# A two-layer decoder trunk on one core: another order of the input, sums of squares in pairs, and a scheduler with three rules more

## The chip, the cores and the metric

The kernel runs on one core of one Trainium2 chip. TensorE (PE in the profile) multiplies matrices and writes into PSUM, eight banks of 512 fp32 values in each of 128 partitions; VectorE (DVE), ScalarE (ACT) and GpSimd (POOL) work on tiles in SBUF, the first two also on PSUM; SyncE (SP) issues the DMA transfers between HBM and SBUF. The engines run side by side, each through its own list of instructions in order, and wait for one another through semaphores. The metric is the device time of one execution in microseconds, as a median of several runs.

## The reference

The input x has 512 rows of 1024 values. Two layers follow one another, then a final RMSNorm. What matters here is the beginning of a layer; the mixers are named alone:

```python
def hybrid_layer(x, c_silu, ...):
    mod = c_silu @ w_ada + b_ada
    shift, scale, gate = jnp.split(mod, 3, axis=-1)
    u = rms_norm(x, norm_g) * (1 + scale[:, None]) + shift[:, None]
    z = u @ w_in
    ...
    ya = dsa_attention(...) * jax.nn.silu(ag)             # indexer, top 128 keys, softmax
    yb = swa_sinks_attention(...) * jax.nn.silu(bg)       # sliding window
    yc = stick_breaking_attention(...) * jax.nn.silu(cg)
    merged = (jax.nn.sigmoid(ma) * (ya @ w_br_a) + jax.nn.sigmoid(mb) * (yb @ w_br_b)
              + jax.nn.sigmoid(mc) * (yc @ w_br_c))
    return x + gate[:, None] * (merged @ w_out)
```

All of it is fp32. z has 8,772 columns per layer.

## The kernel before

**Layout.** Everything is kept transposed: features on the 128 partitions, the 512 rows of x (positions) along the free dimension. x is eight tiles k = 0 to 7 of 128 x 512. A product in fp32 precision is made of three faster ones: each operand is split into a high part (type fp32r) and the low rest, and hi x hi, hi x lo, lo x hi are summed in PSUM. So a weight chunk `wstage` from HBM becomes `whi` (a cast) and `wlo` (a subtraction), and u becomes `uh` and `ul`. `cast` may run on ACT, VectorE or, from SBUF, POOL; `both` (a tensor_tensor) on VectorE or POOL; a line with one engine's name is bound to it.

**Stages of a layer.** `first_phase` multiplies u by the first seven column tiles of w_in (`FIRST`, 896 columns), all seven banks open at once while k runs from 0 to 7: 7 x 3 products per k. `v_phase` makes the value columns. Then several streams are woven into one order: `prep_stream` (the other projections), `mixer_c`, `mixer_ab`, `indexer` and `topk`, `fill_stream` (gates and branch products), `ada_stream` (the next modulation). `out_phase` closes the layer, its last two tiles in two halves of 256 columns.

**The start of layer 0** (`start`, lines 1467 to 1523) loads x in two halves of columns (`norm`): four transfers of two tiles each, then ACT squares them two at a time and 8 products with a matrix of -1 sum the squares over the partitions, which gives -1 times the sum of squares in all partitions; `rstd_of` makes the root through Ln and Exp on ACT, in place in the same PSUM bank. Order of SP's list: small vectors, first half of x, w_ss of k = 0 (`ada_load(0)`, two pieces of 512 KB into Y), the two weight chunks of k = 0, second half of x, w_ss of k = 1, chunks 2 and 3, w_ss of k = 2. `busy` adds products without use that keep TensorE's clock up. Shift and scale of k come from `ada_first(k)`: VectorE multiplies each piece by silu(c), spread over all partitions in `csr`, and sums it along the row; `linear` makes `mods` and `amul`. `times_rstd` (VectorE) multiplies x by the root, `make_u` writes `uh` and a full-precision copy (tile e), both by ACT in layer 0, and `ul` as their difference. The first item of `first_phase` (`two0`) takes k = 0 and 1 together, each in halves of columns, and for each of the seven tiles hi x uh, hi x ul, lo x uh.

**The order.** Nothing of this is emitted at once. Every call is recorded (`Recorder.add`) with its dependencies, taken from overlapping ranges of tiles, and a price for each engine that may run it (`price`). `forward` then builds the whole order as a list scheduler: at each step the engine and the instruction that can start first, ties by due time; `elsewhere` passes an instruction by on one engine when another would end it sooner. `latest` works the due times out backwards from that order. `order` does this five times, each round with the due times of the one before, keeps the round whose modelled end is earliest, and `emit` writes it out. Each engine's instructions keep that order on the chip; the framework adds the semaphores, and it keeps accesses of two engines to one PSUM bank apart whether or not their ranges overlap.

Of the kernel before, what the change touches and what calls it, by code (L numbers as in the profile page):

```python
# [25 lines left out]
F32 = mybir.dt.float32  # L26
# [6 lines left out]
S = 512  # L33
# [216 lines left out]
class Instr:  # L250
    __slots__ = ("i", "alts", "writes", "reads", "preds", "succs", "left", "est", "tiles", "start", "end", "prio", "bound", "engine", "taken", "hold")
# [7 lines left out]
class Recorder:  # L259
# [34 lines left out]
    def add(self, ways):  # L294
        x = Instr()
        x.i = len(self.list)
        op, args, kw = next(iter(ways.values()))
        if op == "pairs":
            named = [(("out", "in", "in")[n], v) for q in args for n, v in enumerate(q[:3])]
            opened = {id(q[0]) for q in args if q[3]}  # L300
        else:
            named = [("out" if "out" not in kw and n == 0 else n, v) for n, v in enumerate(args)] + list(kw.items())
        x.writes = [v for n, v in named if isinstance(v, View) and n in ("out", "accum_out")]
        x.reads = [v for n, v in named if isinstance(v, View) and n not in ("out", "accum_out")]
        x.preds, x.succs = {}, []
        for views, w in ((x.reads, False), (x.writes, True)):
            for v, r in [(v, r) for v in views for r in v.regions()]:
                t = v.tile
                if w and (op == "matmul" and kw["start"] or op == "pairs" and id(v) in opened):
                    r = (r[0], r[1], 0, S)  # L310
                keep = []
                for (j, r2, w2) in t.seen:
                    over = r[0] < r2[1] and r2[0] < r[1] and r[2] < r2[3] and r2[2] < r[3]
                    if over and j is not x and (w or w2):
                        x.preds[j.i] = j
                    if not (w and over and r[0] <= r2[0] and r2[1] <= r[1] and r[2] <= r2[2] and r2[3] <= r[3] and j is not x):
                        keep.append((j, r2, w2))
                t.seen = keep + [(x, r, w)]
        x.tiles = list({id(v.tile): v.tile for v in x.reads + x.writes if not v.tile.pool.fixed}.values())
        for j in x.preds.values():  # L320
            j.succs.append(x)
        x.alts = {}
        for e, (op, args, kw) in ways.items():
            x.alts[e] = self.price(x, e, op, args, kw)
        x.prio = x.i
        self.list.append(x)

    def price(self, x, engine, op, args, kw):
# [67 lines left out]
        y.cost, y.lag = c - self.OVERLAP[engine], c  # L396
        return y


    def forward(self):  # L400
# [3 lines left out]
        for x in self.list:  # L404
            x.left, x.est, x.bound, x.taken = len(x.preds), 0.0, len(x.tiles), False
            for t in x.tiles:
                waiting.setdefault(id(t), []).append(x)
# [6 lines left out]
        def offer(x):  # L414
            if x.left == 0 and x.bound == 0:
                for e in x.alts:
                    heapq.heappush(E[e]["pend"], (x.est, x.i))
# [20 lines left out]
        while len(out) < len(self.list):  # L438
            best = None
            for name, e in E.items():  # L440
# [29 lines left out]
                if mine is not None:  # L470
                    asked = max(free, self.list[mine[2]].est)
                    if best is None or (mine[0], asked, mine) < best[:3]:
                        best = (mine[0], asked, mine, name)
# [43 lines left out]
    def elsewhere(self, x, name, at, E):  # L517

        end = at + x.alts[name].cost
        for o, y in x.alts.items():  # L520
            if o != name:
                t = max(E[o]["free"], at, E[o]["port"] if y.port else 0.0) + y.cost
                if t < end - 1e-9:
                    return True
        return False

    def latest(self, end, out):
# [11 lines left out]
        for x in reversed(out):  # L539
# [4 lines left out]
            if x.engine in after:  # L544
                v = min(v, late[after[x.engine]] - x.hold)
# [59 lines left out]
def trunk(ctx, tc, xT, vecs, w_ss, w_gt, w_first, w_t, w_v, w_br, w_o, rope, consts, out):  # L605
# [146 lines left out]

    def ada_load(j):
        st["wada", j] = [rec.tile("Y", [P, 2 * S], F32) for _ in range(2)]
        for i in range(2):
            SP.dma_start(st["wada", j][i].rearrange("p (a b) -> p a b", a=2), w_ss[0, j, 2 * i:2 * i + 2].rearrange("q p s -> p q s"))
# [54 lines left out]
    def make_u(l, k, xk, cs_=FULL):  # L811
# [5 lines left out]
        for o in (st["uh"][k][:, cs_], t):  # L817
            if l == 0:
# [56 lines left out]
    def stack_q(r, scale=None, sbuf=True):  # L875
        q = rec.tile("Q", [P, 2, S], F32R)
        for e, (a, b) in enumerate(((H0, H1), (H1, H0))):
            if scale is None:
                cast(q[a, e], r[a])
                both(q[b, e], r[a], f(q[a, e]), OP.subtract)  # L880
            else:
                cast(q[a, e], r[a], scale)
# [12 lines left out]
    def stack_k(r, sbuf=True):  # L895
        kh, kl = new_kh(), klow[st["nk"] % 2]
        st["nk"] += 1
        for e, (a, b) in enumerate(((H0, H1), (H1, H0))):
            cast(kh[a, e], r[a])
            cast(kh[b, e], f(kh[a, e]))  # L900
            both(kl[a, :S], r[a], f(kh[a, e]), OP.subtract)
# [50 lines left out]
    def first_phase(l):  # L952
# [19 lines left out]

        def two(*w):
# [493 lines left out]
    def start():  # L1467
# [9 lines left out]
        for h in range(2):  # L1477
# [4 lines left out]
            ACT.activation(csr[:, S * h:S * h + S], p, AF.Copy, scale=-1.0)  # L1482
# [5 lines left out]
        nb = st["nbank"] = st["rstd"] = sbank()  # L1488

        def norm(cs_):  # L1490
            for k in range(0, KT, 2):
                SP.dma_start(xx[k // 4][:, k % 4:k % 4 + 2, cs_], xT[:, k:k + 2, cs_])
            for k in range(0, KT, 2):
                t = t512("t", 10)
                ACT.activation(t.rearrange("p (a b) -> p a b", a=2), xx[k // 4][:, k % 4:k % 4 + 2, cs_], AF.Square)
                for i in range(2):
                    mm(nb[:, cs_], f(nones), t[:, 256 * i:256 * i + 256], cs_.start == 0 and k + i == 0, k + i == 7)
            rstd_of(nb[:, cs_])
# [5 lines left out]
        norm(HALVES[0])  # L1504
        ada_load(0)
        ch.load(1)
# [15 lines left out]
        ch.load(3)  # L1522
# [114 lines left out]
```

## Time and profile before

| | us |
|---|---|
| median of 3 runs | 1181.68 (1181.54 to 1181.86) |
| profiled execution | 1180.98 |
| its span, first to last instruction | 1179.1 |
| mean granted TensorE clock | 0.998 |
| SP's transfers, issue to landing, w_ss pieces of 512 KB | 6.2 |
| SP's transfers, issue to landing, weight chunks of the first projection | 4.4 |

All times of instructions count from the start of the span. In the rows of the profile a line reads: program line, engine, operation, the tile written and the tiles read, shapes, count; then busy microseconds and mean nanoseconds of one, then the engine's idle time before these instructions and what ended it. Nearly all instructions have line 577, since one place emits them, so groups are told apart by tile names: `uh`, `ul`, `whi`, `wlo`, `wstage`; `Y` holds w_ss in the start; `vc` and `va` hold x there; `t` holds squares in the start and softmax tiles later; `ps_z` and `ps_s` are PSUM banks (3 and 5); `small` holds the small vectors. One fp32 product with the matrix of -1 shows as two records.

### The profile page before, as it was taken

Reading aid. Unit: us, or ns where it says so; the run is one execution under the profiler, and the core shown is the slowest. Engines: PE = TensorE matmul, PEld = TensorE weight load, DVE = VectorE, ACT = ScalarE, POOL = GpSimd, SP = SyncE. Lnnn points to the kernel's source line nnn. Section 1 sums busy time; section 2 is a strip of 40 time slices with the busy share of each in tenths; the row PEclk is TensorE's granted clock in tenths of the full one; section 3 lists DMA queues with packets and bytes.
Section 4 is the critical chain, followed back from the end, with each engine's and each line's share of the span. In section 5 each row is a group of like instructions: output and inputs, shape, how many; then the busy total and the mean of one; then the engine's idle time right before and its main releaser. Section 6 shows DMA issues by size and latency. Waiting matters only on the chain.

```text
span 1179.1 us, 17734 instructions
## 1 busy us (share of the span) xinstructions
PE 1166.5 (99%) x6006; PEld 967.9 (82%) x6006; DVE 988.1 (84%) x2275; ACT 532.0 (45%) x1127; POOL 111.8 (9%) x160
## 2 busy tenths in 40 slices
PE   9999999999999999999999999999999999999997
PEld 8899777788878887788899987777888888877886
DVE  6977999999999887787587689999997988667765
ACT  6523667653455532632143147775443653234222
POOL 1100333310000000000000014332100000000000
PEclk9999999999999999999999999999999999999999
DMA  9644323334444454245533432333342333322343
GB/s 354 219 119 120 90 81 86 95 107 125 121 116 126 130 143 143 81 141 153 166 113 108 128 101 72 90 87 119 99 132 83 90 98 100 107 72 88 93 125 106
DMA packets 81914, 139.39 MB, mean 118 GB/s; under 512 B 10016, under 2 KB 22560, under 8 KB 81824
## 3 DMA queue, kind: packets, MB, share of 16 engines
q1 hardware_dynamic: 80672, 136.17, 39.5%
q10 hardware_dynamic: 1152, 2.10, 0.5%
q8 instruction: 47, 0.77, 0.3%
q14 instruction: 43, 0.35, 0.1%
HBM read 125.39 MB, written 4.19 MB: 110 GB/s over the span
## 4 chain that ended last, share of the span: by engine, by line
PE 81%; DVE 13%; ACT 2%; issue 2%; DMA 1%; SPq 0%; DVEq 0%; ACTq 0%
PE ps_z L577 61%; PE ps_s L577 16%; DVE t L577 5%; PE ps_s L575 4%; DVE score L577 2%; ACT t L577 1%; DVE m L577 1%; DVE wlo L577 1%; DVE Q L577 1%; DVE klow L577 1%; DMA Y<-in_w_ss 1%; DVE Y L577 0%; DVE wstage L577 0%; ACT KH L577 0%; ACT e L577 0%
## 5 line engine op out<-in xcount | busy, mean ns | idle before, releaser
L577 PE MATMUL ps_z<-uh,whi 128*128 128x512 f32 (+1 forms) x908 | 357.4, 394 | 0.0
L577 PE MATMUL ps_z<-uh,wlo 128*128 128x512 f32 (+1 forms) x908 | 353.4, 389 | 0.0
L577 PE MATMUL ps_z<-ul,whi 128*128 128x512 f32 (+1 forms) x908 | 352.5, 388 | 0.0
L577 DVE TENSOR_TENSOR wlo<-wstage,whi 128x512 fp32r<-128x512 f32 (+2 forms) x321 | 210.4, 659 | 11.0 <-ACT whi L577 2.3
L577 PEld LDWEIGHTS ps_z<-uh,whi 128*128 128x128 f32 x908 | 170.5, 188 | 35.2 <-issue 1.9
L577 PEld LDWEIGHTS ps_z<-uh,wlo 128*128 128x128 f32 x908 | 170.6, 188 | 34.6 <-issue 0.9
L577 PEld LDWEIGHTS ps_z<-ul,whi 128*128 128x128 f32 x908 | 170.7, 188 | 32.6 <-issue 0.7
L577 DVE CAST whi<-wstage 128x512 fp32r<-128x512 f32 (+2 forms) x224 | 91.3, 408 | 106.6 <-PE ps_z L577 87.5
L577 PE MATMUL ps_z<-Y,whi 128*128 128x512 f32 x384 | 119.3, 391 | 0.0
L577 ACT CAST whi<-wstage 128x512 fp32r<-128x512 f32 (+2 forms) x105 | 63.2, 602 | 109.9 <-PE ps_z L577 82.3
L577 ACT ACTIVATE e<-ps_z 128x512 f32<-128x512 f32 x68 | 40.3, 592 | 135.9 <-PE ps_z L577 135.7
L577 POOL TENSOR_TENSOR wlo<-wstage,whi 128x512 fp32r<-128x512 f32 (+2 forms) x51 | 64.8, 1271 | 382.7 <-ACT whi L577 143.8
L577 ACT ACTIVATE e<-e 128x512 f32<-128x512 f32 x96 | 59.8, 629 | 53.3 <-DVE e L577 52.8
L577 PEld LDWEIGHTS ps_z<-Y,whi 128*128 128x128 f32 x384 | 71.7, 188 | 14.7
L577 ACT ACTIVATE t<-t,nm 128x256 f32<-128x256 f32 (+3 forms) x128 | 65.1, 510 | 35.5 <-DVE nm L577 35.5
L577 PE MATMUL ps_z<-Y,wlo 128*128 128x512 f32 x192 | 74.7, 389 | 0.0
L577 ACT ACTIVATE t<-t 128x512 f32<-128x512 f32 x120 | 68.2, 625 | 13.3 <-DVE t L577 12.5
L577 PEld LDWEIGHTS ps_s<-small,t 128*128 128x128 f32 x432 | 48.8, 140 | 16.2 <-DVE t L577 5.1
L577 PE MATMUL ps_s<-small,t 128*128 128x128 f32 x432 | 58.2, 275 | 3.6 <-DVE t L577 2.5
L577 DVE MAX8 m<-score 128x8 f32<-128x256 f32 (+2 forms) x96 | 53.3, 556 | 1.1
L577 PE MATMUL ps_s<-KH,Q 128*128 128x256 f32 (+3 forms) x280 | 52.4, 309 | 0.2
L577 DVE MATCH_REPLACE8 score<-m,score 128x256 f32<-128x256 f32 (+2 forms) x96 | 52.1, 543 | 0.1
(202 smaller groups left out, 1951.5 us busy)
## 6 DMA issues: line engine op xcount, KB each, us to landing
wstage<-in_w_t SPq DMA_DIRECT2D x212, 256.0 KB, 2.7
wstage<-in_w_v SPq DMA_DIRECT2D x48, 182.0 KB, 2.4
Y<-in_w_ss SPq DMA_DIRECT2D x16, 512.0 KB, 6.2
m<-zs SPq DMA_DIRECT2D x128, 64.0 KB, 2.0
wstage<-in_w_gt SPq DMA_DIRECT2D x32, 256.0 KB, 2.6
wstage<-in_w_ss SPq DMA_DIRECT2D x32, 256.0 KB, 2.7
wstage<-in_w_o SPq DMA_DIRECT2D x32, 256.0 KB, 2.7
wstage<-in_w_first SPq DMA_DIRECT2D x16, 256.0 KB, 4.4
```

What stands on the lines that cost most here:

```text
L575: self.real[engine].matmul(*[real(a) for a in q[:3]], start=q[3], stop=True, skip_group_check=True)
L577: made = getattr(self.real[engine], y.op)(*[real(a) for a in y.args], **{k: real(v) for k, v in y.kw.items()})
```

## The change

The start loads x whole, ahead of everything but the small vectors, in five transfers (2, 2, 2, 1 and 1 tiles); then w_ss of k = 0 (the second piece as two of 256 KB), then chunks 0 and 1. The squares of tiles 0 and 1, of 2 and 3, and of 4, 5 and 6 are added up elementwise before a product sums them; tile 7 goes alone, and the last two sums run in halves of columns. k = 0 is still made in halves, k = 1 whole. In `two0` the products of k = 0 go by term (hi x uh for all seven tiles, then hi x ul, then lo x uh), and k = 1 in full width.

In the recorder three rules come in. Two accesses to one PSUM bank, one of TensorE and one of another engine, now depend on each other even if their ranges don't overlap; two accesses by ACT and VectorE to one bank are kept in their recorded order and, across engines, apart (`after`, `apart`, `soft`). An ACT or VectorE instruction on fewer than 128 partitions is priced as holding its engine for its whole length and a little more. Due times no longer follow the next instruction on the same engine except on PE and SP. `elsewhere` asks when the other engine could start the instruction, rather than from the present one's time on; the modelled landing of early transfers is sooner; and in `stack_q` and `stack_k` the casts are recorded ahead of the subtractions. For k = 0 of layer 0 `make_u` may use VectorE too, and so may the copy into `csr`.

```diff
@@ Recorder.add
+        mine = next(iter(ways)) == "PE"
...
+                bank = t.pool.name[:3] == "ps_"
                 for (j, r2, w2) in t.seen:
                     over = r[0] < r2[1] and r2[0] < r[1] and r[2] < r2[3] and r2[2] < r[3]
-                    if over and j is not x and (w or w2):
+                    if j is not x and (w or w2) and (over or bank and mine != ("PE" in j.alts)):
                         x.preds[j.i] = j
+                    elif j is not x and bank and not mine and "PE" not in j.alts:
+                        x.after[j.i] = j
@@ price
         y.cost, y.lag = c - self.OVERLAP[engine], c
+        if engine != "POOL" and o.shape[0] < P:
+            y.cost = c + (0.08 if engine == "DVE" else 0.02)
@@ forward
-                x.end = dma_free = max(at + 3.0, dma_free) + y.lag * (1.6 if dma_free < 5.5 else 1.0)
+                x.end = dma_free = max(at + (2.1 if at < 20.0 else 3.0), dma_free) + y.lag * (1.2 if dma_free < 5.5 else 1.0)
...
+            for s in x.apart:
+                for o in s.alts:
+                    if o != name:
+                        s.soft[o] = max(s.soft.get(o, 0.0), x.end + self.NEXT)
+                s.left -= 1
+                offer(s)
@@ elsewhere
-                t = max(E[o]["free"], at, E[o]["port"] if y.port else 0.0) + y.cost
+                t = max(E[o]["free"], x.est, x.soft.get(o, 0.0), E[o]["port"] if y.port else 0.0) + y.cost
@@ latest
+            for s in x.apart:
+                v = min(v, late[s.i] - (x.hold if s.engine == x.engine else took + self.NEXT))
-            if x.engine in after:
+            if x.engine in after and x.engine in ("PE", "SP"):
                 v = min(v, late[after[x.engine]] - x.hold)
@@ ada_first
             w = st["wada", j][i]
+            if i > j:
+                for q in range(2):
+                    c = slice(S * q, S * q + S)
+                    DVE.scalar_tensor_tensor(w[:, c], w[:, c], 1.0, csr[:, c], op0=OP.mult, op1=OP.mult, accum_out=o[:, 2 + q:3 + q])
+                DVE.tensor_tensor(out=o[:, 1:2], in0=o[:, 2:3], in1=o[:, 3:4], op=OP.add)
+                continue
@@ make_u
-            if l == 0:
+            if l == 0 and k:
                 ACT.activation(o, xk[:, cs_], AF.Identity, scale=sc, bias=sh)
                 continue
@@ first_phase
+        def terms(w, cs_):
+            fb = st["first"]
+            uh, ul = st["uh"][0][:, cs_], st["ul"][0][:, cs_]
+            for n, v in ((0, uh), (0, ul), (1, uh)):
+                for i in range(NF):
+                    c = slice(128 * (i % 4), 128 * (i % 4) + 128)
+                    mm(fb[i][:, cs_], w[i // 4][n][:, c], v, cs_.start == 0 and n == 0 and v is uh, False)
...
         def two0(*w):
-            for k in (0, 1):
-                for cs_ in HALVES:
-                    mms(k, w[2 * k:2 * k + 2], cs_)
+            for cs_ in HALVES:
+                terms(w[:2], cs_)
+            mms(1, w[2:], FULL)
@@ start
-            ACT.activation(csr[:, S * h:S * h + S], p, AF.Copy, scale=-1.0)
+            cast(csr[:, S * h:S * h + S], p, -1.0)
...
+        for k, n in ((0, 2), (2, 2), (4, 2), (6, 1), (7, 1)):
+            SP.dma_start(xx[k // 4][:, k % 4:k % 4 + n], xT[:, k:k + n])
+        st["wada", 0] = [rec.tile("Y", [P, 2 * S], F32) for _ in range(2)]
+        wada_part(0, 0, 0, 2)
+        wada_part(0, 1, 0, 1)
+        wada_part(0, 1, 1, 1)
+        ch.load(1)
+        for k in range(KT):
+            t = t512("t", 10)
+            ACT.activation(t, x[k], AF.Square)
+            if k in (0, 2, 4):
+                sums = t
+            elif k < 7:
+                both(sums, sums, t, OP.add)
+            if k in (1, 3):
+                mm(nb, f(nones), sums, k == 1, False)
+            if k > 5:
+                for cs_ in HALVES:
+                    mm(nb[:, cs_], f(nones), (sums if k == 6 else t)[:, cs_], False, k == 7)
+        for cs_ in HALVES:
             rstd_of(nb[:, cs_])
...
-        norm(HALVES[0])
-        ada_load(0)
-        ch.load(1)
         busy(3, ch.raw[0][0])
         busy(4, ch.raw[1][0])
         ada_first(0)
-        for k in (0, 1):
-            times_rstd(x[k], HALVES[0])
-            busy(2, x[k])
+        times_rstd(x[0], HALVES[0])
+        busy(2, x[0])
         make_u(0, 0, x[0], HALVES[0])
-        norm(HALVES[1])
+        times_rstd(x[0], HALVES[1])
+        make_u(0, 0, x[0], HALVES[1])
         ada_load(1)
-        for k in (0, 1):
-            times_rstd(x[k], HALVES[1])
+        ch.load(3)
+        times_rstd(x[1])
         ada_first(1)
-        make_u(0, 1, x[1], HALVES[0])
-        make_u(0, 0, x[0], HALVES[1])
-        make_u(0, 1, x[1], HALVES[1])
-        ch.load(3)
+        make_u(0, 1, x[1])
         ada_load(2)
```

More of the change, by code (lines that the diff above doesn't have):

```diff
@@ L250 @@
 class Instr:
-    __slots__ = ("i", "alts", "writes", "reads", "preds", "succs", "left", "est", "tiles", "start", "end", "prio", "bound", "engine", "taken", "hold")
+    __slots__ = ("i", "alts", "writes", "reads", "preds", "succs", "left", "est", "tiles", "start", "end", "prio", "bound", "engine", "taken", "hold", "after", "apart", "soft")
 class Way:
@@ L304, in add @@
         x.reads = [v for n, v in named if isinstance(v, View) and n not in ("out", "accum_out")]
-        x.preds, x.succs = {}, []
+        x.preds, x.succs, x.after, x.apart = {}, [], {}, []
+        mine = next(iter(ways)) == "PE"
         for views, w in ((x.reads, False), (x.writes, True)):
@@ L321, in add @@
             j.succs.append(x)
+            x.after.pop(j.i, None)
+        for j in x.after.values():
+            j.apart.append(x)
         x.alts = {}
@@ L404, in forward @@
         for x in self.list:
-            x.left, x.est, x.bound, x.taken = len(x.preds), 0.0, len(x.tiles), False
+            x.left, x.est, x.bound, x.taken = len(x.preds) + len(x.after), 0.0, len(x.tiles), False
+            x.soft = {}
             for t in x.tiles:
@@ L416, in offer @@
                 for e in x.alts:
-                    heapq.heappush(E[e]["pend"], (x.est, x.i))
+                    heapq.heappush(E[e]["pend"], (max(x.est, x.soft.get(e, 0.0)), x.i))
         def give(c):
@@ L470, in forward @@
                 if mine is not None:
-                    asked = max(free, self.list[mine[2]].est)
+                    asked = max(free, self.list[mine[2]].est, self.list[mine[2]].soft.get(name, 0.0))
                     if best is None or (mine[0], asked, mine) < best[:3]:
@@ L751, in ada_ss, with wada_part @@
         return op(0, lambda w: ada_step(l, j, q, w), (w_ss[l, j, q], True))
+    def wada_part(j, i, q, n):
+        SP.dma_start(st["wada", j][i].rearrange("p (a b) -> p a b", a=2)[:, q:q + n], w_ss[0, j, 2 * i + q:2 * i + q + n].rearrange("q p s -> p q s"))
     def ada_load(j):
@@ L755, in ada_load @@
         for i in range(2):
-            SP.dma_start(st["wada", j][i].rearrange("p (a b) -> p a b", a=2), w_ss[0, j, 2 * i:2 * i + 2].rearrange("q p s -> p q s"))
+            wada_part(j, i, 0, 2)
     def ada_first(j):
@@ L876, in stack_q @@
         q = rec.tile("Q", [P, 2, S], F32R)
-        for e, (a, b) in enumerate(((H0, H1), (H1, H0))):
+        sides = tuple(enumerate(((H0, H1), (H1, H0))))
+        for e, (a, b) in sides:
+            cast(q[a, e], r[a], scale)
+        for e, (a, b) in sides:
             if scale is None:
-                cast(q[a, e], r[a])
                 both(q[b, e], r[a], f(q[a, e]), OP.subtract)
             else:
-                cast(q[a, e], r[a], scale)
                 DVE.scalar_tensor_tensor(q[b, e], r[a], scale, f(q[a, e]), op0=OP.mult, op1=OP.subtract)
@@ L897, in stack_k @@
         st["nk"] += 1
-        for e, (a, b) in enumerate(((H0, H1), (H1, H0))):
+        sides = tuple(enumerate(((H0, H1), (H1, H0))))
+        for e, (a, b) in sides:
             cast(kh[a, e], r[a])
+        for e, (a, b) in sides:
+            both(kl[a, :S], r[a], f(kh[a, e]), OP.subtract)
+        for e, (a, b) in sides:
             cast(kh[b, e], f(kh[a, e]))
-            both(kl[a, :S], r[a], f(kh[a, e]), OP.subtract)
         cast(kl[H1, S:], f(kl[H1, :256]))
@@ L1487, in start @@
         x = st["x"] = [xx[k // 4][:, k % 4] for k in range(KT)]
[L1488 to L1497, printed above, removed]
+        nb = st["rstd"] = sbank()
+        for k, n in ((0, 2), (2, 2), (4, 2), (6, 1), (7, 1)):
[18 more added lines that the diff above has]
+        for cs_ in HALVES:
             rstd_of(nb[:, cs_])
```

## The prediction

> **What bounds the kernel now.** I read the page first: busy time of each engine, then the chain that ended last.
>
> ```profile
> span 1179.1 us, 17734 instructions
> ...
> PE 1166.5 (99%) x6006; PEld 967.9 (82%) x6006; DVE 988.1 (84%) x2275; ACT 532.0 (45%) x1127; POOL 111.8 (9%) x160
> ...
> PE 81%; DVE 13%; ACT 2%; issue 2%; DMA 1%; SPq 0%; DVEq 0%; ACTq 0%
> ```
>
> TensorE is busy for 99% of the span, and the chain is 81% TensorE. The change removes no product of the model itself, so it can win only where TensorE does something else than such products: ahead of the first one, behind the last one, and in holes between. A busy share can hide holes, so next comes the timeline of PE, where starts can be compared (columns: start, duration, instruction, idle time before it).
>
> ```profile
> 11.16 1.76 PE L577 MATMUL ps_s<-wstage,nones 128*128 128x128 f32 x14
> 13.54 0.67 PE L577 MATMUL ps_s<-t,nones 128*128 128x256 f32 x2 [0.62 <-DVE vc L577]
> ...
> 17.77 0.47 PE L577 MATMUL ps_z<-uh,whi 128*128 128x256 f32 x1
> ...
> 18.20 0.28 PE L577 MATMUL ps_z<-uh,wlo 128*128 128x256 f32 x1
> 18.32 0.28 PE L577 MATMUL ps_z<-uh,whi 128*128 128x256 f32 x1
> ...
> 28.03 0.40 PE L577 MATMUL ps_z<-uh,whi 128*128 128x512 f32 x1
> ...
> 51.86 0.39 PE L577 MATMUL ps_z<-uh,whi 128*128 128x512 f32 x1
> 52.08 0.39 PE L577 MATMUL ps_z<-ul,whi 128*128 128x512 f32 x1
> ```
>
> The first product of the first projection starts at 17.77; everything before it is warming and sums of squares. From there a 256-column product starts every 0.12 us and a 512-column one every 0.227 us ((51.86 - 28.03)/105 = 0.227 for the five k of 21 products between the two rows). Tiles k = 0 and 1 take 84 x 0.12 = 10.1 us, then k = 2 begins at 28.03 and k = 7 at 51.86, with hardly a hole. The 13.54 row shows something else: the sums of the second half of the columns waited for VectorE's reading of the first half, in the same PSUM bank.
>
> So the first projection starts late but then runs at TensorE's pace. Whether it can simply be moved forward depends on who feeds it: the table by stretches (for each engine busy us and count, in the order PE, PEld, DVE, ACT, POOL; then granted clock, DMA share, GB/s).
>
> ```profile
> 5.00:10.00 5.00, 5.00 (x15) 3.19 (x15) 0.83 (x2) 2.71 (x5) 0.00 (x0) 1.00 1.03 354
> 10.00:15.00 5.00, 4.38 (x32) 3.90 (x31) 3.81 (x10) 4.19 (x10) 1.00 (x1) 1.00 1.07 387
> 9.20:50.70 41.50, 40.88 (x232) 36.05 (x231) 38.67 (x76) 25.81 (x50) 4.20 (x8) 1.00 0.89 327
> 107.00:230.00 123.00, 121.26 (x641) 94.54 (x640) 120.53 (x248) 78.76 (x144) 40.83 (x58) 1.00 0.30 86
> 1172.30:1179.20 6.90, 0.00 (x0) 0.00 (x0) 2.73 (x8) 0.81 (x2) 0.00 (x0) 0.66 0.43 152
> ```
>
> From 9.2 to 50.7 VectorE is busy 38.67 of 41.5 us: the first projection is fed by an engine that is nearly full, and the DMA engines are full until 15 us. From 107 to 230 VectorE is full again (120.53 of 123). The last 6.9 us hold no product; the diff doesn't touch their operations.
>
> **The change part by part: the start.** What sets the first product is the modulation: both w_ss pieces of k = 0 go through VectorE, give amul, then ACT makes uh, then VectorE ul.
>
> ```profile
> 9.23 1.23 DVE L577 SCALAR_TENSOR_TENSOR Y<-Y,csr 128x1024 f32<-128x1024 f32 x1 [4.17 <-DMA Y<-in_w_ss]
> ...
> 11.86 0.27 DVE L577 TENSOR_SCALAR amul<-dot,small,gb 128x1 f32<-128x1 f32 x1
> ...
> 14.58 0.43 DVE L577 TENSOR_TENSOR ul<-e,uh 128x256 fp32r<-128x256 f32 x1 [1.19 <-ACT e L577]
> ...
> 50.05 0.69 DVE L577 TENSOR_TENSOR ul<-e,uh 128x512 fp32r<-128x512 f32 x1
> ```
> ```profile
> 13.47 0.59 ACT L577 ACTIVATE uh<-vc,mods,amul 128x256 fp32r<-128x256 f32 x1
> ```
> ```profile
> L577 DVE SCALAR_TENSOR_TENSOR wstage<-wstage,csr 128x512 f32<-128x512 f32 x64 | 43.7, 683 | 2.8 <-DMA wstage<-in_w_ss 2.8
> ```
> ```profile
> L577 DVE CAST whi<-wstage 128x384 fp32r<-128x384 f32 x3 | 1.1, 357 | 0.0
> ```
>
> (The last row is the grouping for 9.2 to 50.8 alone.) Before, ul of k = 0 is ready at 15.0, yet the first product waits till 17.77, behind the second half's sums. After, all sums come first, but the other half of x (1.05 MB) also moves ahead of w_ss in SP's queue. At 387 GB/s that is 2.7 us, so VectorE starts on w_ss at 9.23 + 2.7 = 11.9 and not at 9.23. The rows of 9.23 and 11.86 hold two such sums and a cast (0.36) in 2.63 us, so an instruction begins some 0.07 before the one ahead of it ends. After 11.9 come one 1024-wide product sum (1.16 to the next), two 512-wide ones (0.61 each), the new add (0.16, an estimate from the 0.27 of amul, which has one operand more) and amul (0.27): 14.7. uh 0.59 later (it may now go to VectorE too; I keep ACT's row): first product at **15.3**, 2.4 us earlier than now. By term, the seven uh-whi products last 0.84 us to 16.2; ul of that half is then ready (0.5 for the second ACT pass, 0.43). The 42 products of k = 0 end at 20.4. For k = 1 VectorE still has, behind amul, a wlo (0.6, as ul of this shape), ul in two halves (0.7), two w_ss sums (2.3), amul (0.3) and the multiply by rstd (0.6) = 4.5, so 19.2; ACT's two passes and ul (about 2.1) give 21.3, where PE needs it at 20.6. PE waits 0.7, and 21 full-width products (4.77 instead of 5.04) end at 25.9: k = 2 starts **2.1 us earlier** than 28.03, if it is fed.
>
> VectorE's sum over the stretch: it starts at 11.9, and of the 38.67 us I take off 0.3 for 256-wide operations that become whole, 0.55 for casts of weights that ACT could take (half of the x3 row), and add 0.13. That is 37.95, with 0.5 idle (now 41.5 - 38.67 = 2.8) 50.35. Now ul of k = 7 ends at 50.74 and its first use is at 52.08, so 1.3 us of slack are there; leaving 0.15 of it, k = 7 can start 0.4 + 1.2 = **1.6 us earlier**. The smaller of the two counts: the start gains **1.6 us**. If VectorE is never idle and ACT takes all three casts it is 2.6; if VectorE idles 2.8 us as now and keeps its casts, it ends at 53.2, and the start loses 1.3.
>
> Fewer sum products: 32 records of 256 columns go to four 512-wide products' worth. They stand where TensorE waits for w_ss, so they gain nothing beyond the order told above. The three new adds of squares, and csr if VectorE makes it, fall into VectorE's 4.17 us idle in front of 9.23; without that cover the adds would cost 3 x 0.6. SP's queue issues 8 transfers for x and the first w_ss together instead of 10, for the same bytes; nothing waits for an issue there, only for the bytes, and the weights of chunks 0 and 1 move back by the same 2.7 us.
>
> The Trainium skill, DMA: Bandwidth & Descriptors, Bandwidth, gives 341 GB/s for a 1 MB transfer and less for smaller ones. By an estimate from that page x and the first w_ss would come 0.8 us later and the start would gain about 0.8 us. The trace here disagrees: several transfers in flight together moved 354 and 387 GB/s.
>
> **The middle.** The rest of the diff touches only the list scheduler: another order of the same instructions. What can be gained is what TensorE waits there now, from the waits of its weight loads and one such hole:
>
> ```profile
> PEld ps_s L577 <- DVE t L577: 5.1, 12, 0.7
> ...
> PEld ps_s L577 <- ACT t L577: 4.2, 9, 0.9
> ```
> ```profile
> 135.42 0.40 PE L577 MATMUL ps_z<-uh,wlo 128*128 128x512 f32 x1
> 136.46 0.41 PE L577 MATMUL ps_s<-small,t 128*128 128x128 f32 x2 [0.64 <-DVE t L577]
> ```
>
> The hole is 136.46 - 135.42 - 0.23 = 0.8 us. The two rows sum to 9.3 us of idle weight loads, part of it under running products: some **7 us** is the most that a better order could take out. It could add as much. What the new order knows shows in two groups of VectorE that wait for ACT reading the same bank:
>
> ```profile
> L577 DVE TENSOR_TENSOR zc<-ps_z,rt 128x512 f32<-128x512 f32 x28 | 19.1, 684 | 2.2 <-ACT zs L577 2.2
> ...
> L577 DVE TENSOR_SCALAR iw<-ps_s 128x4 f32<-128x4 f32 x8 | 1.3, 160 | 1.9 <-ACT va L577 1.9
> ```
>
> That is 4.1 us of VectorE's time that the old plan didn't foresee. Part of it lies where VectorE is full and TensorE waits for it. I take half, **2.0 us**, as the gain, between 7 gained and 5.5 lost (below). The dearer 64-row steps, the DMA figures and the urgency change only the plan's numbers, not the instructions; their answer is within that same term.
>
> **Sum.** The profiled execution took 1180.98 (span 1179.1 and 1.9 around it). 1180.98 - 1.6 - 2.0 = 1177.4. The three runs' median, 1181.68, stands 0.7 above; I forecast **1178.1** for a median.
>
> **The rivals.**
>
> *The order pays fully* (chance 0.11): most of the 7 us goes, about 5.5, and the start pays 2.6: 1181.7 - 8.1 = 1173.6. For it: the holes are at the same places in both layers, so one cause repaired counts twice. Against it: VectorE is full where they lie.
>
> *It doesn't do what it says* (0.26): the earlier start is eaten by VectorE. If its casts stay and it idles 2.0 us, it ends at 11.9 + 38.5 + 2.0 = 52.4, 1.7 later against 1.2 of slack, and k = 7 starts 0.5 later than now; with 2.0 from the middle that is 1180.2, with none 1182.2. For it: 38.67 of 41.5. Against it: ACT has 15.7 us free there.
>
> *Slower through the new urgency* (0.12): the due time of a VectorE step no longer follows the step behind it, so long work for later (a 0.69 us wlo) can go ahead of a step t that the transposes wait for. There are 24 such groups of steps (12 pairs of heads in each layer). One wlo ahead in eight of them is 8 x 0.69 = 5.5; less the start's 1.6: 1185.6. It turns the sign from three such groups on (3 x 0.69 = 2.1 against 1.6) and passes 0.2% from six on. For it: VectorE full from 107 to 230. Against it: the order is chosen among several rounds.
>
> *The clock drops at the start* (0.04). After the last product the 6.9 us idle show a mean granted clock of 0.66: at half speed for 68% of it, so full speed holds for about 2.2 us of idling. After the change x's last piece stands 0.5 MB behind the place that w_ss's first piece has now (9.23), so it lands near 10.6; a square and two sums (the x2 row of 13.54 among their kind) end near 12.1. The warming products on the weights, now at 11.16, can't begin before 13.9: 1.8 us of idling. That is close. If the clock fell, the 42 products of k = 0 would take up to 5.0 us more: 1183.1. The Trainium skill (TensorE: Matmul & The Clock Gate, Part 1: The HAM clock gate) asks for at least one idle window of about 3.4 us. By that rule 1.8 us is safe and this rival goes.
>
> **How the numbers follow.** Forecast, 1175.5 to 1179.3: 0.47; fully paid 0.11; eaten 0.26; slower 0.12; clock 0.04. About 0.2%, 2.4 us, is what a measurement of this kernel can tell from no change: faster is below 1179.3, slower above 1184.1. Faster 0.47 + 0.11 = 0.58; same 0.26 + 0.04 = 0.30; slower 0.12. The range leaves out the far end of the fully paid case and most of the slower one: **1173 to 1184.5**.
>
> **What would show it.** The first ps_z product with uh at about 15.3, its first seven all uh-whi; k = 2 near 26, k = 7 near 50; VectorE's first Y at about 11.9 and no more than 1 us idle from there to ul of k = 7. From 60 us on, the same places should lie about 1.6 us earlier, and the loads' waits for t should fall from 9.3 by a few us. A later ul of k = 7 than 50.7, or a sum of these waits above 12 us, would prove the forecast wrong; a first Y much before 11.9 would mean that the queue's order cost less than I charge.

## The result, and the profile after

| | before | after |
|---|---|---|
| median, us | 1181.68 (1180.96 to 1181.91) | 1172.77 (1172.66 to 1174.15) |
| ratio after / before | | 0.9927, 95% interval 0.9914 to 0.9941 |
| profiled execution, us | 1180.98 | 1172.66 |
| its span, us | 1179.1 | 1170.5 |

The kernel became 8.9 us faster, where 3.6 were forecast; the time lies 0.2 us below the low end of the range. The page of after, the lines that answer to those shown of before (nearly all instructions now have line 595):

```profile
span 1170.5 us, 17688 instructions
...
PE 1159.6 (99%) x5961; PEld 962.7 (82%) x5961; DVE 985.1 (84%) x2242; ACT 534.3 (46%) x1132; POOL 128.2 (11%) x191
...
PE 96%; DVE 1%; issue 1%; ACT 1%; DMA 1%; SPq 0%; DVEq 0%
```

The busy share of TensorE tells nothing (99% both times). The chain does: TensorE's part went from 81% to 96%, VectorE's from 13% to 1%. So steps of VectorE no longer stand in TensorE's way. The waits of weight loads for `t` say where, first of after:

```profile
PEld ps_s L595 <- DVE t L595: 4.0, 3, 1.9
...
PEld ps_s L593 <- ACT t L595: 1.1, 3, 0.4
```

Before they were 5.1 and 4.2 us, in 12 and 9 waits, 0.8 us of them in the start. The 4.0 that is left is three waits for squares in the start, so of the 8.5 in the middle nothing stayed. The 1.1 belongs to products that another line emits, and answers to this row of before:

```profile
PEld ps_s L575 <- ACT t L577: 1.4, 4, 0.4
```

The stretches, one in each layer, where VectorE is full (columns as in the prediction's table; first after, then the second stretch of before):

```profile
107.00:230.00 123.00, 123.00 (x655) 97.29 (x654) 120.43 (x252) 82.00 (x162) 44.60 (x70) 1.00 0.34 93
684.00:808.00 124.00, 124.00 (x662) 98.06 (x661) 121.77 (x254) 81.42 (x160) 44.65 (x70) 1.00 0.32 92
```
```profile
684.00:808.00 124.00, 122.23 (x646) 95.35 (x645) 121.53 (x256) 78.75 (x145) 41.50 (x58) 1.00 0.30 86
```

TensorE is busy without a gap in both, where 1.7 to 1.8 us were missing before; VectorE is as full as it was, and ACT and POOL do about 3 us more each. Following the same products through both traces (start after minus start before) gives the account:

| same product at (us in before) | 60 | 100 | 240 | 480 | 520 | 660 | 820 | 1160 |
|---|---|---|---|---|---|---|---|---|
| earlier in after by, us | 0.8 | 0.8 | 3.9 | 4.4 | 5.0 | 5.1 | 8.2 | 8.4 |

Between these two executions the start brings 0.8, each of the two stretches 3.1, the rest small holes. The place of the hole that the prediction showed, PE's timeline of after, then VectorE's of before and of after:

```profile
134.23 0.39 PE L595 MATMUL ps_z<-uh,wlo 128*128 128x512 f32 x1
134.46 0.38 PE L595 MATMUL ps_s<-small,t 128*128 128x128 f32 x2
```
```profile
125.34 0.68 DVE L577 TENSOR_TENSOR wlo<-wstage,whi 128x512 fp32r<-128x512 f32 x1
...
131.67 1.22 DVE L577 TENSOR_TENSOR_SCAN t<-ps_s,t 128x511 f32<-128x511 f32 x1
...
132.81 1.20 DVE L577 TENSOR_TENSOR_SCAN t<-ps_s,t 128x511 f32<-128x511 f32 x1
...
135.10 2.32 DVE L577 TENSOR_TENSOR_SCAN t<-ps_s,t 128x511 f32<-128x511 f32 x2
```
```profile
129.51 2.32 DVE L595 TENSOR_TENSOR_SCAN t<-ps_s,t 128x511 f32<-128x511 f32 x2
...
132.93 2.32 DVE L595 TENSOR_TENSOR_SCAN t<-ps_s,t 128x511 f32<-128x511 f32 x2
```

The transposes (`ps_s<-small,t`) need these scans, which are part of mixer c. Before, the third scan ran from 135.10 to about 136.2, and TensorE had reached its place at 135.65: the 0.8 us hole. After, the third scan starts at 132.93, 2.2 us earlier, while TensorE comes there 1.2 earlier; it does not wait. There are four such holes in each layer of before, at 135.4, 161.6, 186.2 and 209.1 in the first: 0.81 + 0.45 + 0.36 + 0.71 = 2.33 us. After has none of them.

The start, PE's timeline of after and VectorE's:

```profile
11.24 1.99 PE L595 MATMUL ps_s<-t,nones 128*128 128x256 f32 x8 [1.03 <-DVE t L595]
13.17 1.83 PE L595 MATMUL ps_s<-wstage,nones 128*128 128x128 f32 x14
...
16.15 0.51 PE L595 MATMUL ps_z<-uh,whi 128*128 128x256 f32 x2
...
26.48 0.62 PE L595 MATMUL ps_z<-uh,whi 128*128 128x512 f32 x2
...
50.33 0.39 PE L595 MATMUL ps_z<-uh,whi 128*128 128x512 f32 x1
50.91 0.50 PE L595 MATMUL ps_z<-ul,whi 128*128 128x512 f32 x1 [0.19 <-DVE ul L595]
```
```profile
9.70 1.49 DVE L595 TENSOR_TENSOR t<-t 128x512 f32<-128x512 f32 x2 [0.66 <-ACT t L595]
11.21 1.23 DVE L595 SCALAR_TENSOR_TENSOR Y<-Y,csr 128x1024 f32<-128x1024 f32 x1
...
14.26 0.27 DVE L595 TENSOR_SCALAR amul<-dot,small,gb 128x1 f32<-128x1 f32 x1
...
15.04 1.34 DVE L595 TENSOR_TENSOR vc<-vc,ps_s 128x256 f32<-128x256 f32 x3
...
50.16 0.69 DVE L595 TENSOR_TENSOR ul<-e,uh 128x512 fp32r<-128x512 f32 x1
```

The first product comes 1.6 us earlier, k = 2 and k = 7 1.5. Then `ul` of k = 7 ends only at 50.85 and the second product starts at 50.91, not at 50.33 + 0.23: a hole of 0.35.

### The profile page after: what moved, and what is told of

Its sections match the earlier page's. It is cut to its first block, busy times and chain, and to the rows that moved or that the text cites. A ratio compares the mean times of both kernels' runs of the same rounds, so it can differ in the third digit from the quotient of the medians.

```text
span 1170.5 us, 17688 instructions
## 1 busy us (share of the span) xinstructions
PE 1159.6 (99%) x5961; PEld 962.7 (82%) x5961; DVE 985.1 (84%) x2242; ACT 534.3 (46%) x1132; POOL 128.2 (11%) x191
## 4 chain that ended last, share of the span: by engine, by line
PE 96%; DVE 1%; issue 1%; ACT 1%; DMA 1%; SPq 0%; DVEq 0%
PE ps_z L595 73%; PE ps_s L595 18%; PE ps_s L593 5%; ACT t L595 1%; DMA va<-in_xT 1%; DVE t L595 0%; DVE Y L595 0%; DVE wlo L595 0%; DVE vc L595 0%; SPq L595 0%; DVE ul L595 0%; ACT e L595 0%; ACT ps_s L595 0%; DVE whi L595 0%; ACT whi L595 0%
## 5 line engine op out<-in xcount | busy, mean ns | idle before, releaser
L595 DVE TENSOR_TENSOR wlo<-wstage,whi 128x512 fp32r<-128x512 f32 (+2 forms) x331 | 218.4, 661 | 12.2 <-ACT whi L595 1.8
L595 DVE CAST whi<-wstage 128x512 fp32r<-128x512 f32 (+2 forms) x233 | 95.5, 410 | 114.2 <-PE ps_z L595 96.0
L595 ACT CAST whi<-wstage 128x512 fp32r<-128x512 f32 (+2 forms) x110 | 66.2, 604 | 131.0 <-PE ps_z L595 106.8
L595 POOL TENSOR_TENSOR wlo<-wstage,whi 128x512 fp32r<-128x512 f32 (+2 forms) x41 | 52.2, 1274 | 144.1 <-DVE whi L595 53.7
```

The costliest lines, as they stand in the source:

```text
L595: made = getattr(self.real[engine], y.op)(*[real(a) for a in y.args], **{k: real(v) for k, v in y.kw.items()})
```

## The experiments

All of them, with the median, and the ratio to before on the same chip (before's medians there are 1181.21 to 1181.48):

| kernel | us | ratio (95%) |
|---|---|---|
| new start, old plan | 1180.97 | 1.0000 (0.9991 to 1.0010) |
| old start, new plan | 1174.11 | 0.9941 (0.9926 to 0.9955) |
| after, without the bank rule | 1176.99 | 0.9964 (0.9951 to 0.9977) |
| after, with the old urgency | 1175.62 | 0.9953 (0.9938 to 0.9968) |
| after, without the 64-row price | 1175.51 | 0.9951 (0.9935 to 0.9968) |
| after, with the old `elsewhere` | 1172.47 | 0.9924 (0.9909 to 0.9939) |
| after, with the old `stack_q`, `stack_k` | 1172.38 | 0.9925 (0.9910 to 0.9939) |
| before, with the 64-row price alone | 1175.80 | 0.9952 (0.9937 to 0.9967) |
| before, with the bank rule alone | 1183.82 | 1.0019 (1.0009 to 1.0028) |
| before, with the new urgency alone | 1180.85 | 0.9995 (0.9986 to 1.0004) |
| before, with a 64-row price far too dear | 1175.71 | 0.9951 (0.9936 to 0.9966) |
| after, three w_ss tiles not summed | 1172.16 | 0.9919 (0.9904 to 0.9934) |

### Start or plan?

The changed kernel with everything undone in the recorder and in `stack_q` and `stack_k`:

```diff
-                    if j is not x and (w or w2) and (over or bank and mine != ("PE" in j.alts)):
+                    if over and j is not x and (w or w2):
...
-        if engine != "POOL" and o.shape[0] < P:
-            y.cost = c + (0.08 if engine == "DVE" else 0.02)
...
-            if x.engine in after and x.engine in ("PE", "SP"):
+            if x.engine in after:
```

> New start (x whole and first, sums in pairs, products of k = 0 by term), old scheduler. The change gained 8.9 us; its trace lies 0.8 us ahead at 60 us and 8.4 at the end, so by the theory that the start pays little and the order in the middle most, this run gains about 0.8 us: 1180.9, and the four holes per layer of 0.4 to 0.8 us ahead of the transposes are still there. By the rival that the start itself brings the whole (an earlier start lets VectorE be ahead of the transposes later), 1173 to 1175.

And the opposite, the changed kernel with the start, `ada_first`, `make_u` and `two0` of before:

```diff
-        for k, n in ((0, 2), (2, 2), (4, 2), (6, 1), (7, 1)):
-            SP.dma_start(xx[k // 4][:, k % 4:k % 4 + n], xT[:, k:k + n])
...
+        norm(HALVES[0])
+        ada_load(0)
+        ch.load(1)
...
-            for cs_ in HALVES:
-                terms(w[:2], cs_)
-            mms(1, w[2:], FULL)
+            for k in (0, 1):
+                for cs_ in HALVES:
+                    mms(k, w[2 * k:2 * k + 2], cs_)
```

> Old start, new scheduler with all its rules. By the theory that the order pays in the middle: gains about 7.6 us, 1174.1, the trace ahead of before by 3 us at 240 us and by 8 at 820. By the rival that start and scheduler need each other (the new due times only help when the start is moved): 1179 to 1182.

The plan alone brings 7.1 us (1181.21 - 1174.11), the start alone nothing. PE's timeline of the start alone:

```profile
42.07 0.73 PE L577 MATMUL ps_z<-uh,whi 128*128 128x512 f32 x2 [0.59 <-ACT uh L577]
...
47.61 0.50 PE L577 MATMUL ps_z<-ul,whi 128*128 128x512 f32 x1 [0.23 <-DVE ul L577]
...
136.91 0.41 PE L577 MATMUL ps_s<-small,t 128*128 128x128 f32 x2 [0.63 <-DVE t L577]
```

The new start meets two new holes inside the first projection, 0.75 and 0.39 us, and the hole before the transposes is as it was. That is the rival "eaten by VectorE" only in part: the smaller hole waits for VectorE's `ul`, the larger for `uh` on ACT. There `uh` starts at 41.20, behind a cast that waited for its weights (ACT's timeline):

```profile
40.68 0.63 ACT L577 CAST whi<-wstage 128x512 fp32r<-128x512 f32 x1 [0.64 <-DMA wstage<-in_w_first]
```

On the new plan the start is worth 1174.11 - 1172.77 = 1.3 us by the medians. The two intervals overlap, so that size is less certain; the two profiles give 1.4 at 60 us (0.6 later than before without the new start, 0.8 earlier with it).

### Which rule: one taken out

The bank rule out of the changed kernel:

```diff
-                    if j is not x and (w or w2) and (over or bank and mine != ("PE" in j.alts)):
+                    if over and j is not x and (w or w2):
                         x.preds[j.i] = j
-                    elif j is not x and bank and not mine and "PE" not in j.alts:
+                    elif False:
```

> The changed kernel without the rule on PSUM banks. If the bank rule brings the middle's gain: back to about 1180.5, with holes of 0.4 to 0.8 us again between 107 and 230 us. If another rule does: 1172 to 1174.

It costs 4.2 us (1176.99 - 1172.77). The four holes stay away; others open. By 60 us the trace is already 1.7 behind the changed kernel's, with holes at 18.4, 22.2 and 42.3 (0.69, 0.81 and 0.63); two more stand at 330.5 and 332.1 (0.57 and 0.73 us, TensorE waits for `mx`). The old urgency:

```diff
-            if x.engine in after and x.engine in ("PE", "SP"):
+            if x.engine in after:
```

> The changed kernel with due times that follow the next instruction of the same engine on all engines again. If urgency by data brings the middle's gain: back to about 1180.5. If the bank rule or the price of 64-row steps does: 1172 to 1174.

It costs 2.9 us, in holes at 487.9, 489.6 and 1064.6 (0.45, 1.35, 1.13), again none of the four. The 64-row price:

```diff
-        if engine != "POOL" and o.shape[0] < P:
-            y.cost = c + (0.08 if engine == "DVE" else 0.02)
```

> The changed kernel without the dearer price of steps on fewer than 128 partitions. The runs without the bank rule and without the urgency rule both kept the middle free of the four holes ahead of transposes, so something else removes them. By the theory of the 64-row price the holes of 0.4 to 0.8 us come back in both layers: 2 x 2.3 us, 1177 to 1178. By the rival (elsewhere, or the casts recorded first) they stay away: 1172 to 1174.

It costs 2.7 us, and here the first of the four places comes back (0.65), the other three do not, and a new hole of 0.83 follows (PE's timeline):

```profile
135.13 0.41 PE L593 MATMUL ps_s<-small,t 128*128 128x128 f32 x2 [0.48 <-DVE t L593]
...
147.10 0.51 PE L593 MATMUL ps_s<-KH,Q 128*128 128x256 f32 x2 [0.57 <-DVE e L593]
```

The second layer has the same two. Each of the three runs lies between the two times that were forecast for it, so no rule carries the middle alone.

Two parts turned out to move nothing, and served as controls:

```diff
-                t = max(E[o]["free"], x.est, x.soft.get(o, 0.0), E[o]["port"] if y.port else 0.0) + y.cost
+                t = max(E[o]["free"], at, E[o]["port"] if y.port else 0.0) + y.cost
```

> The changed kernel with the old question in elsewhere. If this rule removes the four holes: 1177 to 1178 and the holes back between 107 and 230 us. If the 64-row price does: 1172 to 1174.

```diff
-        sides = tuple(enumerate(((H0, H1), (H1, H0))))
-        for e, (a, b) in sides:
-            cast(kh[a, e], r[a])
-        for e, (a, b) in sides:
-            both(kl[a, :S], r[a], f(kh[a, e]), OP.subtract)
-        for e, (a, b) in sides:
+        for e, (a, b) in enumerate(((H0, H1), (H1, H0))):
+            cast(kh[a, e], r[a])
             cast(kh[b, e], f(kh[a, e]))
+            both(kl[a, :S], r[a], f(kh[a, e]), OP.subtract)
```

(and `stack_q` in the same way)

> The changed kernel with stack_q and stack_k recorded as before (each cast followed by its subtraction). If the order of recording matters for the holes: 1175 to 1178. If it only breaks ties: 1172 to 1174.

Both are within 0.4 us of the changed kernel, though of VectorE's some 2,240 instructions about 170 and 330 stand in another place. So these two other orders are worth no microseconds by themselves, and the 2.7 to 4.2 of the three rules are far outside what they show.

### Which rule: one alone

The 64-row price alone, put into the kernel before:

```diff
+        if engine != "POOL" and o.shape[0] < P:
+            y.cost = c + (0.08 if engine == "DVE" else 0.02)
```

> The kernel before with the 64-row price alone. By the theory that this price removes the holes: gains 4 to 5 us, about 1176.5, holes between 107 and 230 us gone. By the rival that any single rule is worth nothing on the old plan: 1180 to 1182, holes in place.

Two lines bring 5.6 us (1181.41 - 1175.80), the largest piece of all. All four holes are gone in both layers, while VectorE waits for ACT in one bank as before (2.9 and 1.9 us, before 2.2 and 1.9). Its first stretch, and one of its VectorE groups:

```profile
107.00:230.00 123.00, 122.92 (x654) 96.74 (x654) 119.33 (x245) 82.06 (x155) 45.88 (x70) 1.00 0.30 90
```
```profile
L579 DVE TENSOR_TENSOR zc<-ps_z,rt 128x512 f32<-128x512 f32 x28 | 19.1, 683 | 2.9 <-ACT zs L579 2.9
```

The bank rule alone:

```diff
+        mine = next(iter(ways)) == "PE"
...
+                bank = t.pool.name[:3] == "ps_"
...
-                    if over and j is not x and (w or w2):
+                    if j is not x and (w or w2) and (over or bank and mine != ("PE" in j.alts)):
                         x.preds[j.i] = j
+                    elif j is not x and bank and not mine and "PE" not in j.alts:
+                        x.after[j.i] = j
```

(with what carries `after`, `apart` and `soft` through `forward` and `latest`)

> The kernel before with the bank rule alone. Taken out of the changed kernel it cost 4.2 us. By the theory that each rule pays by itself: 1177. By the theory that it mends holes that only the new order would have (two of 0.6 and 0.7 us near 331 us, where before had none) and that the 64-row price has to come first: 1179.5 to 1181.5.

It is slower by 2.3 us, outside both forecasts. Its VectorE groups, and its PE timeline:

```profile
L593 DVE TENSOR_TENSOR zc<-ps_z,rt 128x512 f32<-128x512 f32 x28 | 19.1, 681 | 0.0
...
L593 DVE TENSOR_SCALAR iw<-ps_s 128x4 f32<-128x4 f32 x8 | 1.3, 161 | 1.2 <-ACT va L593 1.2
```
```profile
149.55 0.50 PE L593 MATMUL ps_s<-KH,Q 128*128 128x256 f32 x2 [0.93 <-DVE e L593]
...
496.92 1.31 PE L593 MATMUL ps_s<-small,t 128*128 128x128 f32 x10 [1.26 <-DVE t L593]
...
1074.38 1.39 PE L593 MATMUL ps_s<-small,t 128*128 128x128 f32 x10 [0.97 <-ACT t L593]
```

This is the most telling pair of views. The rule does exactly what the prediction credited it with: VectorE's waits for ACT in one bank fall from 2.2 and 1.9 to 0.0 and 1.2, just as in the changed kernel. And the kernel gets slower, because holes of over 1 us open elsewhere, at 148.2, 495.4, 726.4 and 1073.1. The price alone is the counterpart: there the waits stay and the holes go. That VectorE waits less is not a gain; only what TensorE waits for is. (The Trainium skill, PSUM — Partial Sum Buffer, "PSUM bank collisions raise a hardware error", says that software must keep two engines' accesses to one bank and the same 32-partition quadrant apart. That agrees with these waits, which stand in before, 2.2 and 1.9 us, whether or not the plan knows of them.)

The urgency alone:

```diff
-            if x.engine in after:
+            if x.engine in after and x.engine in ("PE", "SP"):
```

> The kernel before with due times by data alone. Taken out of the changed kernel it cost 2.9 us. If it pays by itself: 1178 to 1179.5. If it pays only on a plan that is true otherwise: 1180.5 to 1182.

No difference that can be told (0.9995). The four holes shrink to three, of 0.47, 0.47 and 0.32, but one of 0.98 opens at 58.3, and one of 0.92 at the same place of the second layer.

### Why the 64-row price pays

VectorE's timeline of before, with 128-row instructions first, then 64-row ones:

```profile
56.06 1.28 DVE L577 TENSOR_TENSOR G<-ps_z,e 128x512 f32<-128x512 f32 x2
57.26 0.41 DVE L577 COPY vb<-ps_s 128x256 f32<-128x256 f32 x1
...
171.43 0.68 DVE L577 TENSOR_SCALAR Q<-ps_z 64x512 fp32r<-64x512 f32 x1
172.03 0.67 DVE L577 TENSOR_TENSOR wlo<-wstage,whi 128x512 fp32r<-128x512 f32 x1
172.77 1.39 DVE L577 SCALAR_TENSOR_TENSOR Q<-ps_z,Q 64x512 fp32r<-64x512 f32 x2
174.17 0.09 DVE L577 MATCH_VALUE_LOAD score<-m,score 128x8 f32 x1
```

From start to start the two of 56.06 take 0.60 us each, the two of 172.77 0.70: as a rule the next instruction starts before the end of the one ahead, and at these it does not. But the 64-row cast of 171.43 takes 0.60 like the others. In the whole trace 186 of 212 neighbours of which one has 64 rows don't overlap, 26 do. So the price is about true, and it goes by the wrong thing. The Trainium skill (VectorE: DVE Perf Modes, Two Vector instructions with no wait between them) has a rule that fits: an instruction is held until all earlier ones have finished if an input or its output starts in another group of 32 partitions than the last one there did. By the kernel, a cast such as that of 171.43 reads and writes the same half of the partitions, and in the lower half it starts where 128-row instructions start too; those of 172.77 read one half and write the other. Which half the cast has doesn't show in the trace, so the rows fit this rule and don't prove it.

Is it the truth of the price that pays, or does it pay because it drives these steps from VectorE? A price that is 0.42 us dearer still tells the two apart:

```diff
+        if engine != "POOL" and o.shape[0] < P:
+            y.cost = c + (0.5 if engine == "DVE" else 0.02)
```

> The kernel before with 64-row steps of VectorE priced far too dear (0.58 us over the old price instead of 0.16). If the gain comes from a plan that is true to the chip: this plan sees VectorE late where it isn't, and the time is worse than with the right price (1175.8): 1177 to 1181. If it comes only from moving work off VectorE to ACT and POOL: as good as the right price or better, 1173 to 1176.

It gives the same time as the change's price, 1175.71 against 1175.80. Its first stretch:

```profile
107.00:230.00 123.00, 122.83 (x654) 96.77 (x653) 116.64 (x237) 84.25 (x167) 51.95 (x75) 1.00 0.31 90
```

VectorE's 64 x 512 instructions fell from 137 to 69 in the whole kernel, POOL's rose from 12 to 62. The holes are gone all the same, so "the plan must be true" falls. But with the change's own price alone 135 of the 137 stay on VectorE, so driving these steps away isn't needed either. What is left is that another order, and some other work on ACT and POOL, bring the scans forward. Over all kernels, ACT and POOL together are busy for 117 to 120 us from 107 to 230 where holes stand ahead of the transposes (before 78.76 + 40.83 = 119.6), and for 122 to 136 where none do (after 126.6, the price alone 127.9); a part of that is only that without holes the same window holds more of the program. A cruder measure, VectorE's instructions from the indexer's first product up to the first scan of each of the four groups, does not part the kernels:

| kernel | instructions up to the scan | holes there, first layer, us |
|---|---|---|
| before | 61, 102, 151, 198 | 2.33 |
| before, bank rule alone | 61, 104, 149, 197 | 1.01 |
| after without the 64-row price | 58, 100, 147, 194 | 0.65 |
| before, urgency alone | 57, 97, 142, 189 | 1.26 |
| after, with the old `stack_q`, `stack_k` | 59, 98, 140, 186 | none |
| after, with the old urgency | 56, 94, 144, 191 | none |
| before, 64-row price alone | 57, 96, 140, 190 | none |
| after, without the bank rule | 55, 92, 134, 182 | none |
| after | 55, 95, 141, 186 | none |
| before, price too dear | 53, 89, 132, 180 | none |

TensorE's work up to there is the same in all of them: 96, 168, 240 and 312 products of 512 columns into `ps_z` ahead of the transposes. But the fifth and the sixth row have no holes, and counts that are in part above those of the fourth, which has. Time itself tells more. In the first group TensorE reaches the transposes 30.0 to 30.6 us behind the indexer's first product in every kernel. The third scan ends at 31.0 us in before and at 30.9 with the urgency alone, but at 30.3 with the price alone and at 29.7 in after. So it is shown that the price brings the scans forward, and not which moved instruction does it.

### Does VectorE bind the first projection?

The changed kernel without VectorE's products of w_ss for k = 5, 6 and 7 of the first layer; their shift and scale are taken from k = 4:

```diff
-        o = rec.tile("dot", [P, 4], F32)
-        for i in range(2):
+        o = rec.tile("dot", [P, 4], F32) if j < 5 else None
+        if j > 4:
+            o = st["o4"]
+        st["o4"] = o
+        for i in range(2 if j < 5 else 0):
```

> The changed kernel with the w_ss sums of k = 5, 6 and 7 of layer 0 left out (their shift and scale are those of k = 4): six VectorE sums of 1.15 us less in the first projection, all transfers kept. If VectorE is what takes back half of the start's gain (0.8 us ahead of before at 60 us, where the first products are 1.6 ahead), the hole ahead of k = 7 goes and this run is 0.6 to 0.9 us faster than the changed kernel: about 1172. If the transfers or TensorE set that stretch: 1172.5 to 1173, the hole stays.

The last `ul` now comes at 40.86 instead of 50.16, and the hole at k = 7 is gone. The time, 1172.16, is 0.6 us under the changed kernel's and 0.2 to 0.3 under the two controls'. But the controls, which keep all the sums, lose the hole too. PE's timeline with the old `elsewhere`, where `ul` of k = 7 ends at 50.50:

```profile
50.47 0.40 PE L595 MATMUL ps_z<-uh,whi 128*128 128x512 f32 x1
50.71 0.40 PE L595 MATMUL ps_z<-ul,whi 128*128 128x512 f32 x1
```

From the first product of the first projection to the first `ps_s<-whi,uh` near 56 us TensorE takes 40.09 us in the changed kernel, 39.53 without the three tiles' sums, and 39.54 in both controls. So the hole comes from the place of `ul` in VectorE's list; VectorE's work as such does not bind here.

## Why the prediction was right, and where it was not

**What bounds the kernel: right.** The gain came from holes of TensorE, none of it from TensorE's work in the middle.

**The start's size: about right; its chain: wrong.** Forecast 1.6; measured 1.3 by medians and 1.4 by profiles on the new plan. The first Y came at 11.21, not 11.9, so moving x ahead cost about 2.0 against before's profile instead of 2.7. Yet the first product came at 16.15, not 15.3. The sum ran from Y over `amul` to `uh` and took the root as ready, with the sums of squares ending near 12.1. They ended at 13.23 (the 11.24 row), the roots of both halves, in one bank, followed on ACT until about 15.0, and VectorE's multiplication by the root (`vc<-vc,ps_s`) could begin only at 15.04. `amul` was ready at 14.5. The chain of x itself was late, not that of w_ss. Two things on it were put too low: the adds of squares (four, where the sum counts three) were to fall into idle time, but the last ended at 11.19 and TensorE's last sums began behind it; and these sums, four products in halves, took 2.0 us. That the start's size came out is partly luck: w_ss came 0.7 earlier than charged, the sums of squares 1.1 later.

**VectorE binds at k = 7: right in place, wrong in cause.** k = 7 began at 50.33, forecast as "near 50", and `ul` was late by 0.35. It ended at 50.85, later than the 50.7 that the prediction named as a sign of being wrong. But the sum made the length of VectorE's list the limit, and the two controls make the same sums in another order without that wait. On the old plan the start gains nothing, the outcome of "eaten by VectorE" (0.26); VectorE's own part of it is the smaller hole.

**The middle: the mis-sized term.** Forecast 2.0, measured 7.1. Two steps failed. "I take half" of VectorE's 4.1 us of waits for ACT: those waits did fall to 1.2, but they weren't the cause of the four holes; the rule that takes them away costs 2.3 alone, and the price alone removes the holes with the waits in place. And the dearer 64-row steps "change only the plan's numbers ... their answer is within that same term": they were the largest single piece, 5.6. The bound, "some 7 us is the most that a better order could take out", held by medians (7.1); between 60 and 1160 us the two traces differ by 7.6. "The order pays fully", 0.11, was the case that came. Its 1173.6 lies within 0.8 of the measured time by luck, since of its two terms the order brought 7.1 for 5.5 and the start 1.3 for 2.6. Its argument for (holes at the same places in both layers) outweighed the one against (VectorE is full there): VectorE stayed as full, and its scans came earlier.

**The parts don't add up.** Alone: price -5.6, bank +2.3, urgency -0.6 and start -0.2, both within noise: -4.1. Taken out one by one: 4.2 + 2.9 + 2.7 + 1.3 = 11.1. The whole is 8.9. The bank rule and the urgency pay only with the others. Which pair does it was not tried, nor were the modelled landings of the DMA apart from the rest.

**The rivals that did not come.** The urgency made nothing slower: alone it is within noise, and in the changed kernel it helps. The clock did not drop: TensorE waited 1.03 us ahead of the last sums, warming followed at 13.17 without a gap, and the page shows the clock at 9 tenths or more in every slice. That agrees with the Trainium skill, TensorE: Matmul & The Clock Gate, Part 1, by whose window of about 3.4 us such a wait is too short. The 1.8 us of idling never came, so this rival was not put to the test. The ends of the kernels bear out neither that window nor the prediction's 2.2 us as a bound: over the fourteen profiles the record of the clock falls to half between 1.2 us (old start, new plan) and 4.5 us (without the bank rule) after the last product, in nine of them sooner than 3.4.

## What to carry to other kernels

Where a full engine feeds the bounding one, look for holes that recur at the same places, and don't take only a small share of their sum as the gain of a better order. Here four holes in each of two layers made some 4.7 us, and the rule that removed them brought 5.6 alone. The full engine needed no spare time, only the step waited for earlier in its list. A wait that an off-path engine loses is no gain by itself; check what TensorE waits for. And take the parts of a scheduler change out one at a time as well as putting them in one at a time, since a rule can cost alone what it saves together with others.

## What the runs showed of the hardware

VectorE keeps the 64-row instructions that, by the kernel, read one half of the partitions and write the other apart from the one ahead: 0.70 us instead of 0.60 at 512 columns, by the rows above.

The landing of the first weights varies between executions by some 1.0 us. With the same start code VectorE's first Y stands at 9.23 in the profile of before and here, in that of the 64-row price alone:

```profile
9.98 1.23 DVE L579 SCALAR_TENSOR_TENSOR Y<-Y,csr 128x1024 f32<-128x1024 f32 x1 [5.09 <-DMA Y<-in_w_ss]
```

The four other profiles with the old start have 9.92, 9.98, 10.01 and 10.25; the eight with the new start lie between 11.20 and 12.04. So the profile of before, on which the sum was made, was an early one: the 0.8 us that the start gains between the two profiles understates it.
